# A two-layer transformer trunk: the first products of each feed-forward stage and of its last down units in another order, partial sums in another tile, the norm asked for later

## The chip, the cores and the metric

The kernel runs on 1 core of one Trainium2 chip. The metric is the time of one execution in device microseconds (us), lower is better. A core has five engines that run side by side: TensorE (PE, matmuls; its weight loads are a row of their own, PEld), VectorE (DVE), ScalarE (ACT), GpSimd (POOL) and SyncE (SP), and 16 DMA engines that carry transfers.

## The reference

Each of two layers adds half a feed-forward network, a mixer and half a second feed-forward network to x (512 tokens, 1024 features, D_FF = 2816), all in float32:

```python
def swiglu(x, w_gate, w_up, w_down):
    return (jax.nn.silu(x @ w_gate) * (x @ w_up)) @ w_down
for layer in range(DEPTH):                       # DEPTH = 2
    x = x + 0.5 * swiglu(rms_norm(x, ffn1_norm[layer]), ...)
    x = x + mixer(rms_norm(x, mix_norm[layer]))  # layer 0: pooling and attention; layer 1: gated convolution
    x = x + 0.5 * swiglu(rms_norm(x, ffn2_norm[layer]), ...)
```

The change touches only the four feed-forward networks. They are called stage 1 to stage 4 here; in the trace they lie at about 4 to 365, 555 to 905, 900 to 1250 and 1437 to 1784 us.

## The kernel before

**Data.** Activations are kept transposed, features on the 128 partitions and the 512 tokens along the free dimension. A float32 product is made of three matmuls on split operands: each operand is a high part (cast, ACT, line 87) and a low part (what the cast lost, DVE, line 88), and high times high, high times low and low times high are summed in PSUM (`mm3`, lines 214 to 217, and `product`, lines 461 to 469). Weights arrive by DMA in chunks of 128x1024 and are split in the same way into `whi` and `wlo`, three buffers each; `weights()` (line 203) hands the chunks out in the order in which products ask for them.

**A stage** (`ffn`, line 337). It begins with four "quarters" of plain products of x times the norm's gains (`xs`), 24 matmuls of 128x512 each, for the first gate and up block. Between the first two quarters it asks for the norm: `norm_columns` (line 316: token sums on PE, line 313, then 1/rms on DVE and ACT) and `norm_rows` (line 326: PE spreads the result over the partitions, line 331, and ACT copies it to the tile R, line 333). With R the normalised x (`xn`, line 371) is made, and from it seven right factors with high and low parts, the tiles fB, fT and fN (lines 380 to 400). Then unit 0's gate and up are multiplied by R, passed through silu and multiplied (t and v, lines 447 to 456).

**Units.** All other blocks are done as units of seven products P1 to P7 instead of eight (a scheme of the Strassen kind). The left factor of a product is a sum of weight blocks. The sums are formed in place by accumulating DMAs that POOL issues (line 124): in the tile `sto` P5 (src2 + src3), then P6 (+ src0, after P5 has been split), then P3 (+ src1, after P6 has been split); in the tile `ar` P1 (src0), then P7 (+ src2, after P1 has been split); in tiles `a` P2 and P4, plain loads on SP. P1, P6, P7 and P4 of a unit accumulate in one PSUM bank X, P5 and P3 in Y, P2 in Z. In a gate-up unit X is copied by ACT after P1, P6 and P7 (`copied`, lines 471 to 475): after P1 and P7 to a tile of the tag "R", that is, to the buffer that holds the norm's R at the stage's beginning; the copies are the trace's `x<-bank` at line 474. Down units add each product to x at once (DVE, line 539). In gate-up units and most down units a product has 24 matmuls of 128x256; in units 14 and 15, the two down units of the last group, 18.

**Order.** `staggered` (line 148) writes the products' order by hand: each unit's P5 and P1 lie among the products of the unit before. `full` is 13, the last gate-up unit. Units 14 and 15 are the two down units behind it and need its output: `blocks` makes the factors hz, and a split makes their parts hh (lines 87 and 88) from it. Within that order a list scheduler places instructions of all engines; each engine runs its own list in order. Where a product's weights aren't split in time, PE waits.

Of the kernel before, what the change touches and what calls it, by code (L numbers as in the profile page):

```python
# [10 lines left out]
F32 = mybir.dt.float32  # L11
# [5 lines left out]
P = 128  # L17
D = 1024
T = 512
# [22 lines left out]
def trunk(ctx: ExitStack, tc: tile.TileContext, a, out):  # L42
# [17 lines left out]
    tp = ctx.enter_context(tc.tile_pool(name="tp", bufs=2))  # L60
# [3 lines left out]
    def bank(tag="bank", bufs=None):  # L64
        return pp.tile([P, 512], F32, tag=tag, name=tag, bufs=bufs)

    def held():
        return bank("held", 2)
# [79 lines left out]
    def staggered(kinds, full):  # L148

        order = [(0, "P1"), (0, "P5")]
        for i, kind in enumerate(kinds):
            if i + 1 == len(kinds) or i == full:
                order += [(i, s) for s in ("P6", "P2", "P7", "P3", "P4")]
                order += [(i + 1, s) for s in ("P1", "P5") if i + 1 < len(kinds)]
            else:
                order += [(i, s) for s in ("P6", "P2", "P7")]
                order += [(i + 1, "P5"), (i, "P3"), (i + 1, "P1"), (i, "P4")]
        return order  # L160

    chunks = []
# [1 line left out]
    for l in range(2):  # L164
        for f in ("ffn1", "ffn2"):
# [21 lines left out]
            for kind, p in what:  # L187
                if kind == "gu":
                    units.append(seven([gu[p, q] for q in range(4)], CH, turn))
                else:  # L190
                    gi, e = p
# [4 lines left out]
            order = staggered([k for k, _ in what], max(j for j, (k, _) in enumerate(what) if k == "gu"))  # L196
# [6 lines left out]
    def weights(ahead=3, fetched=6):  # L203
        i = used[0]
        used[0] += 1
        while len(ready) < min(i + ahead, len(chunks)):
            while (loaded[0] < min(max(len(ready) + 1, i + fetched), len(chunks))
                   and chunks[loaded[0]].turn <= now[0]):
                chunks[loaded[0]].load()
                loaded[0] += 1  # L210
            ready.append(chunks[len(ready)].halves())
        return ready[i]

    def mm3(ps, wh, wl, ah, al, start, stop):
        nc.tensor.matmul(ps, wh, ah, start=start, stop=False)  # L215
        nc.tensor.matmul(ps, wh, al, start=False, stop=False)  # L216
        nc.tensor.matmul(ps, wl, ah, start=False, stop=stop)  # L217
# [11 lines left out]
    class Norm:  # L229
        acc = None  # L230
# [65 lines left out]
    def rsqrt(v, n, tag):  # L296

        s = sp.tile([P, n], F32, tag=tag + "s", name="s")
        nc.scalar.activation(s, v, AF.Sqrt)
        r0 = sp.tile([P, n], F32, tag=tag + "r", name="r0")  # L300
        nc.vector.reciprocal(r0, s)
        c = sp.tile([P, n], F32, tag=tag + "c", name="c")
        nc.vector.tensor_mul(c, r0, r0)
        nc.vector.tensor_mul(c, c, v)
        nc.vector.tensor_scalar(c, c, -0.5, 1.5, ALU.mult, ALU.add)
        r = sp.tile([P, n], F32, tag=tag, name="r")
        nc.vector.tensor_mul(r, r0, c)
        return r

    def token_sums(ps, acc):  # L310

        for i in range(NT):
            nc.tensor.matmul(ps[:, 2 * i:2 * i + 2], acc[:, i * P:(i + 1) * P], ones,
                             start=True, stop=True)

    def norm_columns():
        ps = held()
        for sq in Norm.late:
            nc.vector.tensor_add(Norm.acc, Norm.acc, sq)
        Norm.late.clear()  # L320
        token_sums(ps, Norm.acc)
        v = sp.tile([P, NT], F32, tag="nv", name="nv")
        nc.vector.tensor_scalar(v, ps[:, 0:2 * NT:2], 1.0 / D, EPS, ALU.mult, ALU.add)
        return rsqrt(v, NT, "n")

    def norm_rows(r):
        rb = tp.tile([P, NT, P], F32, tag="sq", name="rb")
        nc.vector.tensor_copy(rb, r.unsqueeze(2).broadcast_to([P, NT, P]))
        ps = held()
        for i in range(NT):  # L330
            nc.tensor.matmul(ps[:, i * P:(i + 1) * P], rb[:, i, :], ident, start=True, stop=True)
        R = tp.tile([P, T], F32, tag="R", name="R", bufs=1)
        nc.scalar.copy(R, ps)
        return R, ps


    def ffn(l, f, which, after, first=False):
        what, order = plans[l, f]
        with ExitStack() as es:
# [11 lines left out]
                begin()  # L351
            banks = [bank() for _ in range(4)]

            def quarter(outs, k0, start, stop, cut=None):
                hi, lo = weights()
                for e, ps in enumerate(outs):
                    for i in range(4):
                        s = slice((4 * e + i) * P, (4 * e + i + 1) * P)
                        mm3(ps, hi[:, s], lo[:, s], *xs[k0 + i], start and i == 0, stop and i == 3)

            quarter(banks[0:2], 0, True, False)
            r = norm_columns()
            R, Rp = norm_rows(r)
            quarter(banks[2:4], 0, True, False)
            with tc.tile_pool(name="np", bufs=1) as np_:
                xn = [np_.tile([P, 4, T], F32, tag=f"xn{e}", name=f"xn{e}") for e in range(2)]

# [101 lines left out]
                                         stop=last and i == 2, skip_group_check=True)  # L469

            def copied(ps, name):
                c = tp.tile([P, T], F32, tag="R", name=name, bufs=1) if name == "x1" else \
                    fp.tile([P, T], F32, tag=name, name=name)
                nc.scalar.copy(c, ps)  # L474
                return c
# [567 lines left out]
```

## Time and profile before

| | us |
|---|---|
| median of 3 runs (lowest to highest) | 1786.1 (1782.69 to 1787.74) |
| the profiled execution's own time | 1785.88 |
| its span | 1784.1 |
| PE busy | 1704.7 (96%) |
| PE weight load busy | 1601.1 (90%) |
| DVE busy | 1329.4 (75%) |
| ACT busy | 907.0 (51%) |
| POOL busy | 310.4 (17%) |

The span runs from the first to the last instruction. A matmul's end is modelled, so "PE busy" is not the same as PE at its peak: a PE on a lower clock is busy too. The profile therefore has to be read with the granted clock beside it.

### The profile page before, as it was taken

What the parts mean: (1) busy time and instruction counts of PE and PEld (TensorE: products, weight loads), DVE (VectorE), ACT (ScalarE), POOL (GpSimd) and SP (SyncE); (2) the same over time, 40 slices, a digit from 0 to 9 for tenths busy, and PEclk for the clock granted to TensorE, in tenths of its full rate; (3) what the DMA queues carried; (4) which work ended last, traced back from release to release, by engine and by line L of the source; (5) the groups of instructions that cost most, each with busy time, mean ns of one, the idle gap of its engine ahead of it and who ended that gap; (6) DMA issues with size and microseconds to landing.
All of it is one profiled execution on the core that took longest, in us unless ns stands there. A gap on an engine that the chain in (4) does not pass through costs nothing.

```text
span 1784.1 us, 31312 instructions
## 1 busy us (share of the span) xinstructions
PE 1704.7 (96%) x12642; PEld 1601.1 (90%) x12642; DVE 1329.4 (75%) x1891; ACT 907.0 (51%) x1300; POOL 310.4 (17%) x359
## 2 busy tenths in 40 slices
PE   8899999999999899999989999998999989999997
PEld 6899999878888899999878999998888879999997
DVE  6777786777888877786797867867755677867765
ACT  5564654564655554554555645545322345546452
POOL 2111111124202112111121111112000201111110
PEclk8899999999999899999999999999999989999999
DMA  6689989640015689989657898895332249899985
GB/s 213 157 209 217 223 212 209 141 145 25 19 48 166 154 210 212 220 214 212 143 161 172 214 225 212 209 219 122 107 102 99 95 130 214 211 221 211 222 194 113
DMA packets 89185, 303.19 MB, mean 170 GB/s; under 512 B 10704, under 2 KB 11472, under 8 KB 89040
## 3 DMA queue, kind: packets, MB, share of 16 engines
q0 software_dynamic: 36864, 130.04, 41.5%
q1 hardware_dynamic: 50512, 169.89, 27.0%
q8 instruction: 99, 1.62, 0.4%
q10 hardware_dynamic: 1664, 1.26, 0.2%
q14 instruction: 46, 0.38, 0.1%
HBM read 299.06 MB, written 2.10 MB: 169 GB/s over the span
## 4 chain that ended last, share of the span: by engine, by line
PE 80%; DVE 10%; issue 4%; ACT 3%; DMA 2%; POOL 1%; SPq 0%; ACTq 0%; DVEq 0%; POOLq 0%
PE bank L468 62%; PE bank L216 5%; PE bank L215 5%; PE bank L217 5%; DVE wlo L88 2%; ACT whi L87 1%; DMA sto<-in_ffn_w_gu 1%; DVE xn L371 1%; DVE xs L239 1%; DMA sto<-in_ffn_w_down 1%; DVE x L539 1%; DVE fT L88 1%; DVE fB L88 1%; PE bank L874 0%; PE held L215 0%
## 5 line engine op out<-in xcount | busy, mean ns | idle before, releaser
L468 PE MATMUL bank<-hh,whi 128*128 128x256 f32 x2464 | 434.3, 280 | 15.2 <-ACT whi L87 11.0
L468 PEld LDWEIGHTS bank<-hh,whi 128*128 128x128 f32 x2464 | 377.4, 190 | 19.7 <-ACT whi L87 13.6
L468 PE MATMUL bank<-hh,wlo 128*128 128x256 f32 x1232 | 344.3, 280 | 7.0 <-DVE wlo L88 7.0
L87 ACT CAST whi<-sto 128x1024 fp32r<-128x1024 f32 (+1 forms) x192 | 196.5, 1023 | 289.8 <-PE bank L468 148.7
L468 PE MATMUL bank<-fT,whi 128*128 128x256 f32 x1920 | 341.2, 281 | 0.4 <-ACT x L474 0.4
L88 DVE TENSOR_TENSOR wlo<-sto,whi 128x1024 fp32r<-128x1024 f32 (+1 forms) x192 | 228.7, 1191 | 120.0 <-ACT whi L87 119.0
L468 PEld LDWEIGHTS bank<-fT,whi 128*128 128x128 f32 x1920 | 296.1, 192 | 1.3 <-ACT x L474 1.3
L468 PE MATMUL bank<-fT,wlo 128*128 128x256 f32 x960 | 270.1, 281 | 15.5 <-DVE wlo L88 15.5
L468 PE MATMUL bank<-fN,whi 128*128 128x256 f32 x1280 | 239.0, 289 | 19.7 <-ACT x L474 15.4
L468 PEld LDWEIGHTS bank<-hh,wlo 128*128 128x128 f32 x1232 | 234.4, 191 | 8.9 <-DVE wlo L88 8.9
L468 PEld LDWEIGHTS bank<-fN,whi 128*128 128x128 f32 x1280 | 200.1, 194 | 31.9 <-ACT x L474 20.8
L468 PE MATMUL bank<-fB,whi 128*128 128x256 f32 x1280 | 228.2, 277 | 0.0
L87 ACT CAST whi<-a 128x1024 fp32r<-128x1024 f32 (+1 forms) x128 | 131.2, 1025 | 144.9 <-PE bank L468 87.0
L468 PEld LDWEIGHTS bank<-fT,wlo 128*128 128x128 f32 x960 | 184.0, 192 | 16.3 <-DVE wlo L88 16.3
L468 PEld LDWEIGHTS bank<-fB,whi 128*128 128x128 f32 x1280 | 196.1, 188 | 0.3
L88 DVE TENSOR_TENSOR wlo<-a,whi 128x1024 fp32r<-128x1024 f32 (+1 forms) x128 | 155.1, 1211 | 54.6 <-ACT whi L87 53.8
L124 POOL DMA_DIRECT2D sto<-in_ffn_w_gu x120 | 104.7, 872 | 506.3 <-DVE wlo L88 286.4
L88 DVE TENSOR_TENSOR wlo<-ar,whi 128x1024 fp32r<-128x1024 f32 (+1 forms) x128 | 152.3, 1190 | 48.3 <-ACT whi L87 48.2
L468 PE MATMUL bank<-fN,wlo 128*128 128x256 f32 x640 | 181.2, 283 | 0.0
L87 ACT CAST whi<-ar 128x1024 fp32r<-128x1024 f32 (+1 forms) x128 | 130.9, 1023 | 95.9 <-PE bank L468 52.5
L468 PE MATMUL bank<-fB,wlo 128*128 128x256 f32 x640 | 177.4, 277 | 0.0
L216 PE MATMUL bank<-xs,whi 128*128 128x512 f32 x392 | 155.0, 395 | 2.5 <-DVE xs L239 2.3
(242 smaller groups left out, 2869.6 us busy)
## 6 DMA issues: line engine op xcount, KB each, us to landing
sto<-in_ffn_w_gu POOLq DMA_DIRECT2D x120, 512.0 KB, 7.2
a<-in_ffn_w_gu SPq DMA_DIRECT2D x80, 512.0 KB, 6.6
sto<-in_ffn_w_down POOLq DMA_DIRECT2D x48, 512.0 KB, 7.5
ar<-in_ffn_w_gu SPq DMA_DIRECT2D x40, 512.0 KB, 5.4
sto<-in_ffn_w_gu SPq DMA_DIRECT2D x40, 512.0 KB, 4.6
ar<-in_ffn_w_gu POOLq DMA_DIRECT2D x40, 512.0 KB, 5.4
a<-in_ffn_w_down SPq DMA_DIRECT2D x32, 512.0 KB, 6.0
raw<-in_c_w_in SPq DMA_DIRECT2D x24, 512.0 KB, 3.5
```

The costliest lines, as they stand in the source:

```text
L87: nc.scalar.copy(hi, raw)
L88: nc.vector.tensor_sub(lo, raw, hi.bitcast(F32))
L124: nc.gpsimd.dma_start(out=self.unit[tag], in_=self.srcs[q], accum_op=ALU.add)
L215: nc.tensor.matmul(ps, wh, ah, start=start, stop=False)
L216: nc.tensor.matmul(ps, wh, al, start=False, stop=False)
L217: nc.tensor.matmul(ps, wl, ah, start=False, stop=stop)
L239: nc.vector.scalar_tensor_tensor(xl, x[k], g, xh.bitcast(F32), ALU.mult, ALU.subtract)
L371: nc.vector.scalar_tensor_tensor(xn[e][:, i], x[k], gains[:, which, k:k + 1], R if e else Rp, ALU.mult, ALU.mult)
L468: nc.tensor.matmul(o, w_[:, s], a_, start=fresh and e == 0 and k == 0 and i == 0, stop=last and i == 2, skip_group_check=True)
L539: nc.vector.scalar_tensor_tensor(o, v, 0.5 * sign, o, ALU.mult, ALU.add)
```

## The change

```diff
-        order = [(0, "P1"), (0, "P5")]
+        order = [(0, "P5"), (0, "P1")]
         for i, kind in enumerate(kinds):
-            if i + 1 == len(kinds) or i == full:
-                order += [(i, s) for s in ("P6", "P2", "P7", "P3", "P4")]
-                order += [(i + 1, s) for s in ("P1", "P5") if i + 1 < len(kinds)]
+            if i == full + 1:
+                order += [(i, s) for s in ("P1", "P5", "P2", "P6")]
+                order += [(i + 1, "P5"), (i, "P7"), (i + 1, "P1"), (i, "P3"), (i, "P4")]
             else:
                 order += [(i, s) for s in ("P6", "P2", "P7")]
-                order += [(i + 1, "P5"), (i, "P3"), (i + 1, "P1"), (i, "P4")]
+                if i + 1 == len(kinds) or i == full:
+                    order += [(i, "P3"), (i, "P4")]
+                else:
+                    order += [(i + 1, "P5"), (i, "P3"), (i + 1, "P1"), (i, "P4")]
...
-            def quarter(outs, k0, start, stop, cut=None):
+            def quarter(outs, k0, start, stop, between=None):
                 hi, lo = weights()
                 for e, ps in enumerate(outs):
+                    if e and between:
+                        between()
...
             quarter(banks[0:2], 0, True, False)
-            r = norm_columns()
-            R, Rp = norm_rows(r)
-            quarter(banks[2:4], 0, True, False)
+            rows = []
+            norm = lambda: rows.extend(norm_rows(norm_columns()))
+            quarter(banks[2:4], 0, True, False, None if first else norm)
+            if first:
+                norm()
+            R, Rp = rows
...
-                c = tp.tile([P, T], F32, tag="R", name=name, bufs=1) if name == "x1" else \
+                c = tp.tile([P, T], F32, tag="acc", name=name, bufs=1) if name == "x1" else \
```

Four parts: (1) a stage's first unit begins with P5, then P1, rather than P1, then P5. (2) Unit 14 runs P1 P5 P2 P6, unit 15's P5, P7, unit 15's P1, P3, P4, rather than P1 P5 P6 P2 P7, unit 15's P5, P3, unit 15's P1, P4. (3) X's copies after P1 and P7 go to the tile of the tag "acc", which otherwise holds the norm's sum of squares, rather than to R's. (4) The norm is asked for 12 xs matmuls later, between the halves of the second quarter; in stage 1, 24 later, behind the second quarter. Nothing is computed that wasn't before: the number of instructions is the same on every engine. Lines move by 3 (norm) or 8 (behind line 354).

**ACT at the beginning of stage 2.** `whi<-sto` is the high part of P5's weights, then of P6's, `whi<-ar` of P1's, then of P7's, `whi<-a` of P2's; `x` is X's copy. Before:

```order
L333 COPY R<-held 128x512
L87 CAST whi<-ar 128x1024
...
L87 CAST fT_6293<-hz 128x1024
L87 CAST whi<-sto 128x1024
...
L448 ACTIVATE t<-t 128x512
L87 CAST whi<-sto 128x1024
L448 ACTIVATE t<-t 128x512
L474 COPY x_6536<-bank 128x512
L87 CAST whi<-a_6425 128x1024
```

And with the change:

```order
L87 CAST whi<-sto 128x1024
L336 COPY R<-held 128x512
L87 CAST fB_6292<-xn_6395 128x1024
L87 CAST whi<-ar 128x1024
...
L87 CAST whi<-sto 128x1024
L87 CAST fN_6294<-hz 128x1024
L87 CAST whi<-a_6425 128x1024
...
L87 CAST whi<-ar 128x1024
L482 COPY x_6565<-bank 128x512
```

P5's cast now stands ahead of R's copy, and X's first copy ahead of the silu of t. In stage 3 it is so too; in stage 4 R's copy still comes first, and the cast for P5 next.

**DVE at the same place.** Before:

```order
L371 SCALAR_TENSOR_TENSOR xn_6395<-x,gains,held 128x512 x4
...
L397 SCALAR_TENSOR_TENSOR hz<-hz,xn_6396 128x1024
L88 TENSOR_TENSOR wlo<-sto,whi 128x1024
L447 TENSOR_TENSOR t<-bank,R 128x512
L88 TENSOR_TENSOR fT_6298<-hz,fT_6298 128x1024
L450 TENSOR_TENSOR v<-bank,R 128x512
...
L88 TENSOR_TENSOR wlo<-sto,whi 128x1024
```

And with the change:

```order
L88 TENSOR_TENSOR wlo<-sto,whi 128x1024
L379 SCALAR_TENSOR_TENSOR xn_6395<-x,gains,held 128x512 x4
...
L405 SCALAR_TENSOR_TENSOR hz<-hz,xn_6396 128x1024
L455 TENSOR_TENSOR t<-bank,R 128x512
L458 TENSOR_TENSOR v<-bank,R 128x512
L88 TENSOR_TENSOR fT_6298<-hz,fT_6298 128x1024
L88 TENSOR_TENSOR wlo<-sto,whi 128x1024
```

P5's low part has gone from behind line 397 to ahead of xn, and P6's, the second `wlo<-sto`, from behind both halves of the gating to behind one t, one v and one fT. In stage 4 P1's low part (`wlo<-ar`), in stages 2 and 3 among the factors, stands behind the last hz (line 405).

**DVE at unit 14 of stage 1**, where its first products meet the last gate-up unit's output; `a1` is P2's tile. Before:

```order
L439 SCALAR_TENSOR_TENSOR hz_3575<-hz_3575 128x256
L539 SCALAR_TENSOR_TENSOR x_76<-bank_3727,x_76 128x2x256
L88 TENSOR_TENSOR hh_3686<-hz_3575,hh_3686 128x512
L88 TENSOR_TENSOR wlo_3732<-sto_3577,whi_3731 128x768
L88 TENSOR_TENSOR wlo_3757<-a1_3646,whi_3756 128x768
L539 SCALAR_TENSOR_TENSOR x_76<-bank_3755,x_76 128x2x256
L88 TENSOR_TENSOR wlo_3782<-ar_3543,whi_3781 128x768
```

And with the change:

```order
L447 SCALAR_TENSOR_TENSOR hz_3575<-hz_3575 128x256
L88 TENSOR_TENSOR wlo_3732<-a1_3612,whi_3731 128x768
L88 TENSOR_TENSOR hh_3686<-hz_3575,hh_3686 128x512
L547 SCALAR_TENSOR_TENSOR x_76<-bank_3730,x_76 128x2x256
L88 TENSOR_TENSOR wlo_3758<-sto_3577,whi_3757 128x768
L547 SCALAR_TENSOR_TENSOR x_76<-bank_3754,x_76 128x2x256
L88 TENSOR_TENSOR wlo_3783<-sto_3692,whi_3782 128x768
```

P2's low part, from a plain load, now comes first, P6's third, and unit 15's P5 (`sto_3692`) ahead of P7's `ar`.

## Rows read from the trace of the kernel before

**Rows 1.** The page's part 4: the chain that ended last, by engine.

```profile
PE 80%; DVE 10%; issue 4%; ACT 3%; DMA 2%; POOL 1%; SPq 0%; ACTq 0%; DVEq 0%; POOLq 0%
```

**Rows 2.** PE's waits: us in total, times, longest us.

```profile
PE bank L468 <- DVE wlo L88: 22.5, 13, 4.2
PE bank L468 <- ACT x L474: 15.8, 12, 4.1
PE bank L468 <- ACT whi L87: 11.0, 13, 1.5
PE held L313 <- DVE acc L319: 8.9, 3, 6.7
```

**Rows 3.** Timeline of PE, stages' beginnings: start us, us, what, [idle before <-releaser].

```profile
586.98 0.58 PE L468 MATMUL bank<-fT,wlo 128*128 128x256 f32 x1 [4.16 <-DVE wlo L88]
...
595.10 0.80 PE L468 MATMUL bank<-fN,whi 128*128 128x256 f32 x2 [3.77 <-ACT x L474]
...
945.29 0.57 PE L468 MATMUL bank<-fN,whi 128*128 128x256 f32 x1 [3.19 <-ACT x L474]
...
1469.84 0.58 PE L468 MATMUL bank<-fN,whi 128*128 128x256 f32 x1 [3.11 <-ACT x L474]
```

**Rows 4.** Timeline of DVE, beginning of stage 2.

```profile
567.93 2.72 DVE L371 SCALAR_TENSOR_TENSOR xn<-x,gains,held 128x512 f32<-128x512 f32 x4 [2.85 <-ACT R L333]
...
584.57 1.22 DVE L397 SCALAR_TENSOR_TENSOR hz<-hz,xn 128x1024 f32<-128x1024 f32 x1
585.71 1.21 DVE L88 TENSOR_TENSOR wlo<-sto,whi 128x1024 fp32r<-128x1024 f32 x1
586.84 0.68 DVE L447 TENSOR_TENSOR t<-bank,R 128x512 f32<-128x512 f32 x1
...
594.08 1.22 DVE L88 TENSOR_TENSOR wlo<-sto,whi 128x1024 fp32r<-128x1024 f32 x1 [2.56 <-ACT whi L87]
```

**Rows 5.** Timeline of ACT, beginning of stage 2.

```profile
567.31 0.59 ACT L333 COPY R<-held 128x512 f32<-128x512 f32 x1 [4.03 <-PE held L331]
...
593.00 1.04 ACT L87 CAST whi<-sto 128x1024 fp32r<-128x1024 f32 x1 [4.19 <-DMA sto<-in_ffn_w_gu]
...
594.48 0.57 ACT L474 COPY x<-bank 128x512 f32<-128x512 f32 x1
```

**Rows 6.** Timeline of DVE, xn of stage 3.

```profile
918.04 1.41 DVE L371 SCALAR_TENSOR_TENSOR xn<-x,gains,held 128x512 f32<-128x512 f32 x2 [2.43 <-ACT R L333]
```

**Rows 7.** Windows, stage 2: PE, PEld, DVE, ACT, POOL busy, clock, DMA, GB/s.

```profile
572.00:576.00 4.00, 4.00 (x20) 3.30 (x19) 4.00 (x6) 2.11 (x2) 0.00 (x0) 1.00 0.54 107
```

**Rows 8.** The tile sto, 555 to 600 us (its DMA issues; time to landing).

```profile
L124 POOL DMA_DIRECT2D sto<-in_ffn_w_gu x4: 866/876/917, 565.3 to 595.7; - x4
...
DMA to landing us min/median/max: 5.2/6.5/9.5
```

**Rows 9.** Timeline of PE, the tail of stage 1 (units 14 and 15).

```profile
335.16 0.51 PE L468 MATMUL bank<-hh,whi 128*128 128x256 f32 x2 [0.82 <-ACT whi L87]
336.42 0.51 PE L468 MATMUL bank<-hh,whi 128*128 128x256 f32 x2 [0.75 <-ACT whi L87]
337.28 0.39 PE L468 MATMUL bank<-hh,wlo 128*128 128x256 f32 x1 [0.35 <-DVE wlo L88]
...
361.60 0.38 PE L468 MATMUL bank<-hh,wlo 128*128 128x256 f32 x1 [1.54 <-DVE wlo L88]
```

**Rows 10.** Timeline of ACT, P6's cast in unit 14 of stage 1.

```profile
334.28 0.83 ACT L87 CAST whi<-sto 128x768 fp32r<-128x768 f32 x1 [2.75 <-DMA sto<-in_ffn_w_down]
```

**Rows 11.** Windows in the tail of stage 1, columns as in rows 7.

```profile
338.00:342.00 4.00, 4.00 (x24) 4.00 (x24) 2.81 (x5) 0.83 (x1) 0.74 (x1) 0.60 0.78 158
342.00:346.00 4.00, 4.00 (x37) 4.00 (x36) 2.66 (x5) 1.67 (x2) 0.87 (x1) 1.00 0.65 112
334.30:361.60 27.30, 23.83 (x184) 23.17 (x183) 22.29 (x27) 14.76 (x21) 8.43 (x8) 0.94 0.54 112
```

**Rows 12.** The tile sto, 326 to 366 us.

```profile
DMA to landing us min/median/max: 4.5/5.2/5.8
```

## Prediction before the run

> **What bounds the kernel now.** I read the chain that ended last first: 80% of it is PE, 10% DVE [rows 1]. So the time is PE's work plus the places where PE waits. The list of PE's waits names those: 22.5 us for low parts (DVE, line 88), 15.8 us for X's copies (line 474), 11.0 us for high parts (ACT, line 87), 8.9 us in three waits of the token sums (line 313), one of them 6.7 us [rows 2]. PE's timeline then says where they lie. Two lie at each stage's beginning: P5's first matmul waits for its low part (4.16 us in stage 2), and P6's for X's copy (3.77, 3.19 and 3.11 us in stages 2 to 4) [rows 3]. The other cluster lies in each tail, where unit 14's P6 and P2 wait 0.82, 0.75 and 0.35 us, and unit 15's P3 waits 1.54 us at the end [rows 9]. Last I read the granted clock in windows of the tail: 0.60 from 338 to 342 us, just behind the three waits, where 24 matmuls are recorded in 4.00 us; 1.00 in the next four, with 37 [rows 11]. A gap is thus paid a second time in slow matmuls behind it. The change aims at both clusters; the reader should judge each by its own stage.
>
> The sum is made against the profiled execution, 1785.9 us with a span of 1784.1; it lies 0.2 us under the median of the three runs, so no correction is made.
>
> **The tails (part 2).** Before, P6 comes first of the products that need the last gate-up unit's output. Its weights are the last to be ready: its accumulating DMA had to wait for P5's split, its cast on ACT starts at 334.28 after 2.75 us of waiting for that DMA [rows 10]. DVE then splits P6 and only then P2, and PE, whose first wait begins at 335.16 - 0.82 = 334.34, ends both products' first pieces at 337.3 [rows 9]. By the window that follows, 24 matmuls fit from 338 to 342 [rows 11]; with the four early ones and some four between 337.3 and 338, 32 of the 36 are done by 342.0, all by about 342.6.
>
> After, P2 comes first. Its weights are a plain load, and DVE splits them before the last hh. P6 has P2's 18 matmuls as cover for its cast and split, done by about 336.1 by the same durations. With no wait, 36 matmuls at 4.00/37 = 0.108 us take 3.9 us from 334.34: 338.2. The gain is 342.6 - 338.2 = 4.4; I take 4.3. It costs nothing elsewhere: the same DMAs, casts and splits are issued, and the end wait of P3 is already there.
>
> What is late next is DVE. From 334.3 to 361.6, 27.3 us, DVE is busy 22.3 us and PE 23.8 us [rows 11]; PE's part holds about 1.4 us of slow clock (13 matmuls of 0.108 us that didn't fit between 338 and 342). So this stretch can't fall below about 22.3 on either engine: at most 5.0 can be won in it. The second thing that may be late is P3 of unit 14. Its DMA is issued when P6 is split, and between P6 and P3 lie three products (5.8 us at 0.108), against a landing of 4.5 to 5.8 us plus a cast and a split of nearly 1 us each [rows 12]. That is a tie within some 2 us. The bounds are therefore 2 and 5 per tail, against 4.3 as the likeliest, nearer to the top because the matmuls that wait are known and the tie is within the slack of P7. Four tails: 17.2, from 8 to 20.
>
> **The beginnings (parts 1, 3 and 4).** Before, P6 of stage 2 starts at 595.10 and xn at 567.93 [rows 3, 4]: 27.2 us, and in stage 3 945.29 - 918.04 = 27.2 too [rows 3, 6]. DVE runs without a break in between: the chain of factors to 585.71, then P5's low part, then the gating's t and v; P5's split starts P6's DMA, P6's cast waits 4.19 us for it until 593.00, and X's copy stands behind that cast on ACT, at 594.48 [rows 4, 5]. X's copy before also needed R free, so it couldn't go ahead of the gating.
>
> After, P5 is split ahead of xn and P6's DMA lands during the factors. P6 then needs P6's low part, which stands behind the factors (585.71 - 567.93 = 17.8 us), one t and one v (0.6 each with overlap), a fT and its own split (1.2 each) [rows 4]: 21.3 us behind xn. X's copy has no tie to R any more. If xn stayed where it is, each stage would win 27.2 - 21.3 = 5.9 us. But xn moves.
> - **Stage 1**: the norm stands behind 24 more xs matmuls. At 4.00/20 = 0.2 us each [rows 7] that is 4.8 us; one token sum still stands where it stood, so the 6.7 us wait remains [rows 2]. Its remaining slack of 1.1 us I count as 0.2, since the stage's first matmuls also wait for their first loads. Bounds 0 and 1.1.
> - **Stage 3**: 12 more xs matmuls cost 2.4; the wait ahead of line 313, of which stages 2 and 3 have 8.9 - 6.7 = 2.2 between them [rows 2], goes. Net +0.9 to +1.3. P5's cast comes ahead of R's copy here too, but ACT waits for 4 us at that place (4.03 in stage 2 [rows 5]), and in this stage POOL has little ahead of the DMA, so I take the cast to fit in. Gain 5.0; bounds 4 and 5.4, the cast being late is E.
> - **Stage 2**: P5's cast stands ahead of R's copy on ACT. P5's DMA was issued at 565.3 [rows 8]; with its load first on SP I put it 2 us earlier, 563.3. A landing took 5.2 to 9.5 us [rows 8], so the cast ends at 569.5 to 573.9 and R's copy follows instead of standing at 567.31 [rows 5]. xn moves by 2.3 to 6.6 us; I take 5.9, as the transfers at this place are the slow ones. Gain 0; bounds -0.7 and 3.6.
> - **Stage 4**: R's copy still comes first, but P1's split stands behind all factors: 18.9 us behind xn. P7's DMA follows (5.2 to 6.5 [rows 8]), then its cast (1.0) and, behind it on ACT, X's copy (0.6): 25.7 to 27 us. With xn 1.4 later and five matmuls of P2 drawn ahead (0.5 us), the result is -0.5; bounds -1.5 and 2.
>
> Sum 0.2 + 0 + 5.0 - 0.5 = 4.7, from about 2 to 12.
>
> Part 3 by itself costs nothing: the tag's old user, the norm's sum, is read last before the factors begin, and the next norm's sums start when the gate-ups are done. P1 and P5 swapped adds no work either.
>
> **Sum.** 17.2 + 4.7 = 21.9; 1785.9 - 21.9 = **1764.0**.
>
> **One rule against the change.** POOL's DMAs in the tail landed in 4.5 to 5.8 us while DVE was busy 22.3 of 27.3 us [rows 11, 12], so a busy DVE did not visibly hold them. The Trainium skill ("SBUF — State Buffer", the box on DVE blocking a DMA) says that a DMA issued by GpSimd can starve for descriptors while VectorE holds the port the two share. A tail that is denser on DVE would then make every accumulating DMA later, which is case B by another road; the rows speak against it so far.
>
> **The rivals.**
> - **B, the tails give half back.** P3 of unit 14 and the last P3 wait for DVE and for the accumulating DMA, so that only 2 us per tail remain: 8 + 4.7 = 12.7, 1773. For it: the tie above, and DVE at 22.3 of a possible 23. Against it: the landings in this tail are short [rows 12]. Chance 0.17.
> - **C, everything comes at its upper bound.** Tails 4 x 5 = 20, beginnings 12: 32, 1754. For it: stage 2's landing could be as short as 5.2 us, the shortest of that tile. Chance 0.18.
> - **D, no change that a measurement can tell** (within 0.3%, 5.4 us; a run of this kernel can't tell less). The order of PE's waits only changes: unit 14's P6 waits in its new place as long as P6 and P2 did, and P6 of the stages starts 27 us behind xn for another reason, the DMA of P7. 1784. Against it: P2's weights need no DMA sum. Chance 0.06.
> - **E, slower.** ACT's cast of P5 holds R's copy, and with it xn and everything behind it, until an accumulating DMA lands. It decides when that DMA delays R's copy by over 13.7 us more than I take it to in each of stages 2 and 3, since 2 x 13.7 = 27.3 is the forecast gain and 5.4 more. At 17 us: 1764 + 34 = 1798. No landing in the rows took more than 9.5 us [rows 8]. Chance 0.04.
>
> **How the numbers follow.** A, the forecast, has 0.55, with a range of its own from 1758 (tails 5.0, beginnings 8) to 1770 (tails 3.3, beginnings 2.7). To hold 8 in 10 the range takes in C's centre and most of B: 1754 to 1776. Faster by over 0.3% are A, B and C: 0.90; within 0.3% D: 0.06; slower E: 0.04.
>
> **What would show it right or wrong.** Tails: no wait over 0.5 us between P1 and P7 of unit 14, and a clock of 1.00 behind it. Beginnings: P6 starts 21.3 us behind xn in stages 1 to 3, and about 26 in stage 4; the token sums' wait shrinks from 8.9 to 6.7. In stage 2 ACT waits for `sto` ahead of R's copy. Wrong would be: a wait of over 2 us ahead of unit 14's P3; P6 still waiting for X's copy in stage 3; R's copy in stage 3 held by P5's cast.

## The result

The changed kernel took 1765.7 us (median of 4 runs, 1761.67 to 1768.79) where the kernel before took 1786.9 us beside it (median of 4, 1782.69 to 1788.9): a ratio of 0.9883, 95% interval 0.9855 to 0.9911. That is 1.2% faster; the forecast was 1764.0 in a range of 1754 to 1776. The profiled execution of the changed kernel is the slowest of its four, 1768.79 us, so the profiled spans differ by 17.1 us where the medians differ by 21.2.

The head of the page after, which answers to the table of before:

```profile
span 1767.0 us, 31319 instructions
...
PE 1697.0 (96%) x12642; PEld 1594.4 (90%) x12642; DVE 1328.1 (75%) x1891; ACT 906.9 (51%) x1300; POOL 312.0 (18%) x359
```

No engine does less work. PE's waits after (us in total, times, longest), beside [rows 2]:

```profile
PE bank L476 <- DVE wlo L88: 15.8, 8, 4.8
PE bank L476 <- ACT x L482: 11.2, 13, 3.2
PE bank L476 <- ACT whi L87: 6.8, 8, 1.0
PE held L316 <- DVE acc L322: 6.7, 1, 6.7
PE bank L476 <- DVE t L455: 4.1, 2, 3.6
```

The low parts' share falls from 22.5 to 15.8 us, the high parts' from 11.0 to 6.8, X's copies' from 15.8 to 11.2; a new one, for the gating's t, comes with 4.1.

**The tails.** PE's timeline of stage 1's tail after, beside [rows 9]:

```profile
332.24 0.39 PE L476 MATMUL bank<-hh,whi 128*128 128x256 f32 x1 [0.45 <-DVE hh L88]
...
357.60 0.39 PE L476 MATMUL bank<-hh,wlo 128*128 128x256 f32 x1 [1.58 <-DVE wlo L88]
```

Between the wait for the last factors at 332.24 and the last P3 there is none; the waits of 0.82, 0.75 and 0.35 us are gone. The windows of this tail (columns as in rows 7):

```profile
333.00:337.00 4.00, 4.00 (x36) 3.87 (x35) 3.51 (x7) 2.39 (x4) 0.00 (x0) 1.00 0.67 165
337.00:341.00 4.00, 4.00 (x35) 3.97 (x35) 4.00 (x6) 1.48 (x2) 1.75 (x2) 1.00 0.54 76
334.70:357.60 22.90, 21.30 (x183) 20.76 (x182) 20.60 (x27) 13.45 (x19) 9.15 (x8) 1.00 0.64 133
```

The clock stays at 1.00 where it was 0.60 for four us before, and 36 matmuls fit in four us where 24 did. The stretch from the first matmul behind unit 14's P1 and P5 to the last P3, 27.3 us before [rows 11], is 22.9 here with as many matmuls (183 against 184). DVE is busy for 20.6 us of it, against 22.3 of the longer stretch. P3's wait for DVE, 1.58 us, stands where one of 1.54 stood.

**The beginnings.** Stage 2 after, on ACT, DVE and PE:

```profile
571.88 1.05 ACT L87 CAST whi<-sto 128x1024 fp32r<-128x1024 f32 x1 [8.44 <-DMA sto<-in_ffn_w_gu]
572.96 0.59 ACT L336 COPY R<-held 128x512 f32<-128x512 f32 x1
...
623.31 1.05 ACT L87 CAST whi<-sto 128x1024 fp32r<-128x1024 f32 x1 [3.43 <-DMA sto<-in_ffn_w_gu]
```

```profile
574.11 2.72 DVE L379 SCALAR_TENSOR_TENSOR xn<-x,gains,held 128x512 f32<-128x512 f32 x4
...
594.23 1.22 DVE L88 TENSOR_TENSOR wlo<-sto,whi 128x1024 fp32r<-128x1024 f32 x1
```

```profile
591.79 0.80 PE L476 MATMUL bank<-fN,whi 128*128 128x256 f32 x2 [3.19 <-ACT x L482]
595.50 0.58 PE L476 MATMUL bank<-fN,wlo 128*128 128x256 f32 x1 [2.08 <-DVE wlo L88]
610.36 0.51 PE L476 MATMUL bank<-fT,whi 128*128 128x256 f32 x2 [1.03 <-ACT whi L87]
625.41 0.50 PE L476 MATMUL bank<-fT,whi 128*128 128x256 f32 x2 [1.39 <-ACT x L482]
```

ACT waits 8.44 us for P5's accumulating DMA with R's copy behind it; xn starts at 574.11. P6's split starts 20.1 us behind xn and ends 21.3 behind it, as computed, and P6's bulk runs from 595.50, where the whole of P6 ran from 595.10 before [rows 3]. Behind it two more waits follow, 1.03 and 1.39 us, both put down to ACT, which the kernel before didn't have there. In the second ACT is held again: its cast at 623.31 waits 3.43 us for an accumulating DMA, and X's copy stands behind that cast. Stage 3, where nothing holds R's copy, shows the same 20.1 us on DVE; P6's bulk there is 21.4 us behind xn, 5.9 less than P6 before [rows 3, 6]. P6's first two matmuls there still wait for X's copy, 2.30 us (3.19 before [rows 3]):

```profile
918.11 2.72 DVE L379 SCALAR_TENSOR_TENSOR xn<-x,gains,held 128x512 f32<-128x512 f32 x4
...
938.23 1.22 DVE L88 TENSOR_TENSOR wlo<-sto,whi 128x1024 fp32r<-128x1024 f32 x1
```

```profile
935.62 0.51 PE L476 MATMUL bank<-fN,whi 128*128 128x256 f32 x2 [2.30 <-ACT x L482]
...
939.50 0.58 PE L476 MATMUL bank<-fN,wlo 128*128 128x256 f32 x1 [2.07 <-DVE wlo L88]
```

**The balance.** The timelines of PE and DVE give a ledger. A beginning is counted from the end of the last product matmul of the stage before (for stage 1 from 0) to the first add to x of a down unit (line 539 before, 547 after), so those of stages 2 and 4 hold the mixers. A tail is counted from the last gate-up matmul to the end of the last product. All in us of the profiled executions; the rest of the span is the body of the stages.

```
                    beginnings, stages 1 to 4       sum   tails, stages 1 to 4       sum    span
before              129.5  303.0  113.1  289.4    835.0   37.1  37.0  36.7  38.2   149.0  1784.1
after               128.7  309.7  109.7  288.3    836.4   32.4  32.3  32.8  30.6   128.1  1767.0
tail_alone          127.9  302.4  112.8  288.2    831.3   32.3  32.2  32.4  30.2   127.1  1756.6
begin_alone         128.9  305.2  109.5  289.1    832.7   36.6  36.1  35.8  33.7   142.3  1774.3
p6_first            128.3  308.2  109.5  287.2    833.1   36.5  36.4  36.4  35.2   144.5  1776.4
swap_only           129.1  302.4  114.5  289.1    835.1   33.8  33.2  33.6  33.0   133.6  1769.2
p1_first            130.5  299.5  110.8  289.7    830.6   32.3  32.8  32.1  30.3   127.4  1758.5
copies_r            131.2  305.1  110.7  286.9    833.9   32.3  32.2  32.4  30.1   126.9  1762.6
late_alone          131.8  299.0  111.4  291.6    833.7   36.3  36.9  36.1  34.4   143.6  1780.6
tail_acc            129.0  301.5  111.9  289.5    831.8   32.2  32.3  32.3  31.0   127.8  1758.1
norm_early          125.2  301.9  112.5  285.2    824.8   32.3  32.3  32.1  30.0   126.7  1749.9
early_r             125.0  299.3  109.8  284.7    818.8   32.9  32.9  32.8  30.9   129.5  1745.8
hybrid              127.2  299.5  109.7  289.0    825.4   32.3  32.3  32.2  29.9   126.7  1753.9
best                124.5  298.1  109.7  286.6    818.9   32.2  32.2  32.2  30.0   126.5  1748.1
```

From before to after, the tails win 20.9 us, the beginnings lose 1.4 and the rest 2.4: together the 17.1 by which the span is shorter. So the change is its tails. How far such rows can be trusted is seen in kernels that share a part. Tails of the new order agree within 1.1 us. Those of the four kernels with P6 ahead of P2 agree within 1 us in stages 1 to 3, but in stage 4 the kernel before has 38.2 where begin_alone, late_alone and p6_first have 33.7 to 35.2. The beginnings of one arrangement differ by up to 4 us in the sum, and the rest, in which the kernels differ only by the tile of X's copies, lies between 797.5 and 803.3. Stage 2's beginning holds the mixer of layer 0, which was slower in this execution after (in the last section).

### The profile page after: what moved, and what is told of

It is laid out like the page before. It is cut to its first block, busy times and chain, and to the rows that moved or that the text cites. A ratio compares the mean times of both kernels' runs of the same rounds, so it can differ in the third digit from the quotient of the medians.

```text
span 1767.0 us, 31319 instructions
## 1 busy us (share of the span) xinstructions
PE 1697.0 (96%) x12642; PEld 1594.4 (90%) x12642; DVE 1328.1 (75%) x1891; ACT 906.9 (51%) x1300; POOL 312.0 (18%) x359
## 3 DMA queue, kind: packets, MB, share of 16 engines
q1 hardware_dynamic: 50512, 169.89, 27.2%
## 4 chain that ended last, share of the span: by engine, by line
PE 80%; DVE 10%; issue 3%; ACT 3%; DMA 3%; POOL 1%; SPq 0%; ACTq 0%; DVEq 0%; POOLq 0%
PE bank L476 61%; PE bank L218 5%; PE bank L219 5%; PE bank L220 5%; DMA sto<-in_ffn_w_gu 2%; DVE wlo L88 2%; ACT whi L87 1%; DVE xn L379 1%; DVE xs L242 1%; DVE fT L88 1%; DVE fB L88 1%; PE bank L882 0%; PE held L218 0%; PE held L219 0%; PE held L220 0%
## 5 line engine op out<-in xcount | busy, mean ns | idle before, releaser
L476 PE MATMUL bank<-hh,whi 128*128 128x256 f32 x2464 | 429.9, 278 | 7.3 <-ACT whi L87 3.9
L476 PEld LDWEIGHTS bank<-fT,whi 128*128 128x128 f32 x1920 | 292.1, 189 | 11.2 <-ACT whi L87 3.5
```

The costliest lines, as they stand in the source:

```text
L476: nc.tensor.matmul(o, w_[:, s], a_, start=fresh and e == 0 and k == 0 and i == 0, stop=last and i == 2, skip_group_check=True)
```

## The experiments

Each comparison is with the kernel before on the same chip; ratios carry their 95% interval. Edits are against the changed kernel, except where the text says that they are against the kernel before.

**1. The tail's order alone** (tail_alone): the kernel before with the loop of `staggered` that the change has, and nothing else.

```diff
...
+            if i == full + 1:
+                order += [(i, s) for s in ("P1", "P5", "P2", "P6")]
+                order += [(i + 1, "P5"), (i, "P7"), (i + 1, "P1"), (i, "P3"), (i, "P4")]
...
```

> Only part 2 (the order of unit 14's products) is put into the kernel before. Theory: the tails carry the whole gain, because P2's plain load is ready while P6's accumulating DMA, cast and split run under P2's matmuls. Then PE has no wait between P1 and P7 of unit 14, the tails are shorter by 4.0 to 4.7 us in stages 1 to 3 and about 7 in stage 4 as in the changed kernel, and the time is about 1766 us (1762 to 1770). Rival: the beginnings (P5 first, copies in acc, late norm) carry it, and the tail's gain is given back to DVE: 1780 us or more.

Measured: 1766.4 us, 0.9885 (0.9863 to 0.9907), as the whole change. The tails sum to 127.1 us, 21.9 less than before. The theory holds: the tails alone are worth what the whole change is worth.

**2. The beginnings alone** (begin_alone): parts 1, 3 and 4 with the order of unit 14 as before.

```diff
-            if i == full + 1:
...
+            if i + 1 == len(kinds) or i == full:
+                order += [(i, s) for s in ("P6", "P2", "P7", "P3", "P4")]
...
```

> Parts 1, 3 and 4 (P5 first, copies in the acc tile, late norm) without part 2. Theory: what stages 3 and 4 win (about 5 us together) stage 2 loses, where R's copy waits on ACT behind P5's cast for the accumulating DMA: 1787 us (1783 to 1790), and the three waits of each tail are back. Rival (beginnings carry the gain): 1775 us or less.

Measured: 1778.3 us, 0.9959 (0.9944 to 0.9975): between the two, 4.7 us under the theory's range. The beginnings themselves give 2.3 us (835.0 to 832.7), and R's copy is held as in the changed kernel:

```profile
571.41 1.05 ACT L87 CAST whi<-sto 128x1024 fp32r<-128x1024 f32 x1 [8.55 <-DMA sto<-in_ffn_w_gu]
572.48 0.59 ACT L333 COPY R<-held 128x512 f32<-128x512 f32 x1
```

But the tails, whose order is the old one, are 6.7 us shorter too, 4.5 of them in stage 4. The tile sto's time to landing there, before and in this kernel:

```profile
DMA to landing us min/median/max: 4.7/4.7/8.0
```

```profile
DMA to landing us min/median/max: 4.2/4.9/6.1
```

A landing of 8.0 us, which the last products of before waited for, is missing. Why it landed late there, and whether it does so in every execution, is open: there is one profile of the kernel before. If it does, it would explain why the parts don't add: 19 us by the tail alone and 7 by the beginnings alone, but 21 together, since either part takes stage 4's late landing off the path. That is argued and not shown.

**3. P6 ahead of P2 again** (p6_first):

```diff
-                order += [(i, s) for s in ("P1", "P5", "P2", "P6")]
+                order += [(i, s) for s in ("P1", "P5", "P6", "P2")]
```

> The changed kernel with P6 ahead of P2 in unit 14 again, unit 15's P5 still ahead of P7. Theory: the waits for P6's cast and split come back ahead of P6 and P2, 1.9 us per tail with the slow clock behind them, and the time is 1777 to 1783 us. Rival: the gain comes from unit 15's P5 and P1 being drawn forward, by which the accumulating DMAs of unit 15 start earlier: 1764 to 1770 us as the changed kernel.

Measured: 1776.7 us, 0.9946 (0.9924 to 0.9967), 0.3 us under the theory's range and far from the rival's. The waits are back in stage 1's tail:

```profile
333.51 0.50 PE L476 MATMUL bank<-hh,whi 128*128 128x256 f32 x2 [0.58 <-ACT whi L87]
334.76 0.50 PE L476 MATMUL bank<-hh,whi 128*128 128x256 f32 x2 [0.75 <-ACT whi L87]
335.49 0.67 PE L476 MATMUL bank<-hh,whi 128*128 128x256 f32 x2 [0.23 <-ACT whi L87]
...
359.49 0.39 PE L476 MATMUL bank<-hh,wlo 128*128 128x256 f32 x1 [1.65 <-DVE wlo L88]
```

and the tails sum to 144.5 us, 16.4 more than after. With the same beginnings and unit 15's P5 behind P7, begin_alone has 142.3 us of tails and 0.9959: unit 15's P5 drawn ahead of P7 brings nothing by itself.

**4. P2 and P6 exchanged and nothing more** (swap_only), against the kernel before:

```diff
...
+                order += [(i, s) for s in ("P1", "P5", "P2", "P6")]
+                order += [(i, "P7"), (i + 1, "P5"), (i, "P3"), (i + 1, "P1"), (i, "P4")]
...
```

> The kernel before with nothing but P2 put ahead of P6 in unit 14; unit 15's P5 and P1 stay where they were, behind P7 and P3. Theory: the exchange of P2 and P6 alone is the tail's gain; PE has no wait between P1 and P7 of unit 14, the tails are about 32.5 us each and the time is 1766 us (1762 to 1771). Rival: unit 15's P5 drawn ahead of P7 is needed too, since P7 then comes 18 matmuls too early for its split; a wait ahead of P7 or P3 stands in the tails and the time is 1772 to 1778 us.

Measured: 1774.1 us, 0.9935 (0.9914 to 0.9956). Here the rival was right. The tails sum to 133.6 us: the exchange wins 15.4 of the 21.9 us that tail_alone wins, and PE still waits ahead of P7 and, a little longer than before, ahead of the last P3:

```profile
338.46 0.38 PE L471 MATMUL bank<-hh,wlo 128*128 128x256 f32 x1 [0.49 <-DVE wlo L88]
357.73 0.38 PE L471 MATMUL bank<-hh,wlo 128*128 128x256 f32 x1 [1.81 <-DVE wlo L88]
```

The wait ahead of P7, 0.3 to 0.5 us, stands in all four tails; with unit 15's P5 ahead of P7 (run 1) it stands in none. Both halves of part 2 are needed.

**5. P1 first** (p1_first):

```diff
-        order = [(0, "P5"), (0, "P1")]
+        order = [(0, "P1"), (0, "P5")]
```

> The changed kernel with P1 ahead of P5 at a stage's beginning again (part 1 undone). Theory: in stage 2 ACT casts P1's plain load ahead of R's copy and waits for no accumulating DMA; the 8.4 us wait of ACT goes, xn starts some 5 us earlier and P6 with it, stage 3 stays as it is, stage 4 loses 1 to 3 us since P6 stands behind both halves of the gating again: 1760 us (1757 to 1765). Rival: P5 first is what shortens the beginnings, and without it P6 is 27 us behind xn everywhere: 1770 to 1775 us.

Measured: 1763.3 us, 0.9877 (0.9859 to 0.9896): in the theory's range, though the ratios don't tell it from the changed kernel. On ACT in stage 2 the cast ahead of R's copy waits for no DMA now:

```profile
562.07 1.05 ACT L87 CAST whi<-ar 128x1024 fp32r<-128x1024 f32 x1 [2.30 <-PE bank L219]
563.83 0.59 ACT L336 COPY R<-held 128x512 f32<-128x512 f32 x1 [0.70 <-PE held L334]
```

and stage 2's beginning falls from 309.7 to 299.5. Stages 1 and 4 lose 1.8 and 1.4, stage 3 loses 1.1.

**6. Copies in R's buffer** (copies_r), part 3 undone:

```diff
-                c = tp.tile([P, T], F32, tag="acc", name=name, bufs=1) if name == "x1" else \
+                c = tp.tile([P, T], F32, tag="R", name=name, bufs=1) if name == "x1" else \
```

> The changed kernel with X's copies after P1 and P7 back in R's buffer (part 3 undone). Theory: X's copy must wait until both halves of the gating have read R, which stand behind P6's and P2's splits now, so P6 starts later than its split allows, some 27 to 30 us behind xn in stages 1 to 3 instead of 21; 2 to 6 us per stage are lost: 1772 us (1768 to 1780). Rival: the acc tile does nothing, since P6 waits for its low part anyway: 1765.7 us as the changed kernel, within 2.

Measured: 1765.1 us, 0.9886 (0.9859 to 0.9912), the same as the changed kernel. The theory falls, though the delay that it named is there: P6's bulk is 25.7 to 26.0 us behind xn in stages 1 to 3, 4.3 to 4.6 more than after. PE runs more of P2 meanwhile, and no time is lost. Part 3 is worth nothing that can be measured, and how far P6 stands behind xn doesn't by itself set the time.

**7. The norm asked for early** (norm_early), part 4 undone:

```diff
-            quarter(banks[2:4], 0, True, False, None if first else norm)
-            if first:
-                norm()
-            R, Rp = rows
+            R, Rp = norm_rows(norm_columns())
+            quarter(banks[2:4], 0, True, False)
```

> The changed kernel with the norm asked for between the first two quarters again (part 4 undone). Theory: R's copy stands ahead of P5's cast on ACT, xn in stage 2 starts where it did before (about 202 us behind stage 1's end, 7 us earlier than in the changed kernel without the mixer's share), but X's copy stands behind P7's cast, whose DMA starts only after the factors, so P6 starts 26 us behind xn in stages 2 to 4: stage 2 wins 2 to 5 us, stage 3 loses 2 to 4, 1765 us (1761 to 1769). Rival: the late norm is what shortens stages 2 and 3, so that without it the time is 1770 us or more.

Measured: 1753.1 us, 0.9821 (0.9795 to 0.9848), 12 us under the theory's 1765, 8 under its range, and clear of the changed kernel's interval: both expectations missed. Part 4 costs the changed kernel some 11 us by the ratios: the beginnings sum to 824.8 us against 836.4, by 3.5 us less in stage 1, 7.8 in stage 2, 3.1 in stage 4, and 2.8 more in stage 3.

**8. A beginning chosen for each stage** (hybrid): stages 1 and 4 as before, stage 2 with P1 first, copies in acc and the late norm, stage 3 as in the changed kernel.

```diff
+                              ("P5", "P1") if (l, f) == (1, "ffn1") else ("P1", "P5"))
...
+                c = tp.tile([P, T], F32, tag="acc" if which in (2, 3) else "R", name=name, bufs=1) if name == "x1" else \
...
+            late = which in (2, 3)
+            if not late:
+                norm()
+            quarter(banks[2:4], 0, True, False, norm if late else None)
...
```

> Each stage's beginning is chosen from the runs so far: stages 1 and 4 as before (P1 first, copies in R, early norm), stage 2 with P1 first, copies in acc and the late norm, stage 3 as in the changed kernel; the tails as in the changed kernel. Theory: the stages' gains add, since each beginning is bounded by its own chain from xn: about 3 us in stage 2 and 3 in stage 3 over the tails alone (1766.4), 1760 us (1756 to 1763). Rival: what a stage wins at its beginning it gives back in waits for splits and copies of the next units, or runs vary by more than this: 1763 us or more.

Measured: 1755.9 us, 0.984 (0.9814 to 0.9866): just under the theory's range. Stage 2's beginning is that of run 5 (299.5), stage 3's that of the changed kernel (109.7), and those of stages 1 and 4 are within 0.8 us of run 1: the stages' beginnings add within what they vary by.

**9. The late norm alone** (late_alone), part 4 put into the kernel before.

```diff
-            r = norm_columns()
-            R, Rp = norm_rows(r)
-            quarter(banks[2:4], 0, True, False)
+            rows = []
+            norm = lambda: rows.extend(norm_rows(norm_columns()))
+            quarter(banks[2:4], 0, True, False, None if first else norm)
+            if first:
+                norm()
+            R, Rp = rows
```

> The kernel before with nothing but the late norm (part 4). Theory: asking later delays xn by 5 us in stage 1 and by about 1 us in each other stage, and P6 stays 25 to 27 us behind xn since X's copies wait for R; what is left is the delay: 1790 us (1787 to 1795). Rival: the late norm only hurts together with P5 first, whose cast on ACT then stands ahead of R's copy; alone it is free: 1783 to 1786 us.

Measured: 0.9983 (0.9967 to 0.9999), 1778.6 us where the kernel before took 1782.3 beside it. The theory's loss isn't there; the rival's "alone it is free" fits, though the time is 4.4 us under its range too; the kernel before was 3.4 us or more faster here than beside runs 1 to 8. In stage 2 R's copy isn't held, since P1's plain load is cast ahead of it, and stage 2's beginning is 299.0; stage 1 loses 2.3 and stage 4 2.2.

**10. Parts 2 and 3** (tail_acc): P1 first, early norm, copies in acc.

```diff
-        order = [(0, "P5"), (0, "P1")]
+        order = [(0, "P1"), (0, "P5")]
...
+            R, Rp = norm_rows(norm_columns())
+            quarter(banks[2:4], 0, True, False)
...
```

> Parts 2 and 3 alone: the tail's order and X's copies in acc, with P1 first and the early norm. Theory: with P1 first P5's split stands behind all factors, P6's DMA starts only then and P6 is 27 us behind xn as before, wherever X's copy goes: 1766 us as the tail alone (1762 to 1769), 13 more than with P5 first. Rival: it is X's free copy and not P5 first that brought the early-norm kernel to 1753: 1752 to 1757 us.

Measured: 1761.2 us, 0.9878 (0.9859 to 0.9897). By the ratio this is the tail alone, as the theory had it; its 1761 is 0.8 us under the stated range, and the kernel before was 3.6 us faster beside it than beside tail_alone. The copy's buffer isn't what brought norm_early to 1753.

**11. Parts 1 and 2** (early_r): P5 first and the tail's order, the norm early, the copies in R.

```diff
-                c = tp.tile([P, T], F32, tag="acc", name=name, bufs=1) if name == "x1" else \
+                c = tp.tile([P, T], F32, tag="R", name=name, bufs=1) if name == "x1" else \
...
+            R, Rp = norm_rows(norm_columns())
+            quarter(banks[2:4], 0, True, False)
...
```

> Parts 1 and 2 alone: P5 first and the tail's order, with the early norm and X's copies in R (the early-norm kernel with part 3 undone). Theory: P6's split still ends some 22.5 us behind xn, X's copy moves only by one silu on ACT (0.6 us) because it already stood behind P7's cast; beginnings lose under 1 us per stage: 1754 us (1751 to 1758). Rival: the copy's buffer matters, P6 falls back to 27 us or more behind xn: 1762 us or more.

Measured: 1750.4 us, 0.9818 (0.98 to 0.9836), 0.6 under the range. It beats both kernels and is smaller than the change. The step of the theory was wrong all the same: in stage 2 P6's split ends 24.8 us behind xn and not 22.5, and P6 starts 29.3 behind it, as the rival had it, without costing what the rival said. PE's timeline of stage 2 first:

```profile
569.65 0.38 PE L472 MATMUL bank<-fT,wlo 128*128 128x256 f32 x1 [0.24 <-DVE wlo L88]
578.74 0.58 PE L472 MATMUL bank<-fB,wlo 128*128 128x256 f32 x1 [6.08 <-DVE wlo L88]
584.01 0.38 PE L472 MATMUL bank<-fB,wlo 128*128 128x256 f32 x1 [0.28 <-DVE wlo L88]
586.61 0.51 PE L472 MATMUL bank<-fN,whi 128*128 128x256 f32 x2 [0.50 <-ACT x L478]
```

Then the windows from P5's first matmul over 36 us, of this kernel and of the changed one (columns as in rows 7):

```profile
569.00:605.00 36.00, 28.71 (x219) 27.30 (x218) 33.80 (x45) 22.88 (x30) 6.09 (x7) 0.91 0.61 140
```

```profile
579.80:616.00 36.20, 28.40 (x195) 27.25 (x196) 32.84 (x43) 20.26 (x26) 4.34 (x5) 0.81 0.45 98
```

There is one long wait, 6.08 us, in P1, where the changed kernel has four: 2.22 and 1.36 us in P5, 3.19 and 2.08 at P6. While X's copy and P6's split are still being made, PE runs 18 of P2's 24 matmuls; P6 waits 0.50 us and all its 24 matmuls follow in one piece. In the changed kernel only two of P2's matmuls stand there, and P6 is torn into 2 and 22 with a wait on each side. So 219 matmuls are done in 36.0 us against 195 in 36.2, at a mean clock of 0.91 against 0.81. DVE is busy 33.8 of the 36.0 us.

P2's matmuls ahead of P6 aren't what decides, though. The four kernels with P5 first and the new tails, by norm and by the tile of X's copies (counts and distances in stage 2, P6 from its third matmul on):

```
                          P2's matmuls   P6 behind   xn behind         beginnings,
                          ahead of P6    xn          stage 1's end     sum           ratio
after       late, acc           2          21.4        212.4             836.4       0.9883
copies_r    late, R            10          25.7        208.7             833.9       0.9886
norm_early  early, acc          5          29.4        201.1             824.8       0.9821
early_r     early, R           18          29.6        201.3             818.8       0.9818
```

The ratio goes with the norm, that is, with xn, and neither with the order of P2 and P6 nor with P6's distance from xn. What early_r has over norm_early in the beginnings, 6.0 us of two executions, its ratio doesn't show.

**12. A beginning chosen for each stage, with P5 first in stages 1 and 4** (best): hybrid with stages 1 and 4 as in norm_early.

```diff
+                              ("P1", "P5") if (l, f) == (0, "ffn2") else ("P5", "P1"))
...
+            late = which in (2, 3)
+            if not late:
+                norm()
+            quarter(banks[2:4], 0, True, False, norm if late else None)
...
```

> The early-norm kernel in stages 1 and 4 (P5 first, acc, norm as before), stage 2 with P1 first and the late norm, stage 3 as in the changed kernel; tails as in the changed kernel. Theory: stages add: 2.4 us in stage 2 and 2.8 in stage 3 over the early-norm kernel by the profiled beginnings: 1749 us (1745 to 1752). Rival: the stages' differences of 2 to 3 us are within what one kernel varies by from run to run: 1752 to 1757 us.

Measured: 1750.8 us, 0.983 (0.9811 to 0.9849). By the median it is in the theory's range, but no better than early_r, whose two parts do the same without a choice by stage.

## Why the prediction was right, and where it wasn't

**The sum** came out, in part by luck: 21.9 us were forecast, 21.2 measured between medians. Its two terms were off in opposite directions. In the profiled executions the tails gave 20.9 us, not 17.2; the beginnings lost 1.4 where 4.7 were to be won; the rest, which had no term, lost 2.4.

**The tails.** The mechanism is shown by runs 1, 3 and 4: P2's plain load is ready, and its matmuls cover P6's DMA, cast and split. In all four tails the waits of P6 and P2 are there in each kernel with P6 ahead of P2 and in none with P2 ahead. 4.3 us per tail were forecast; stages 1 to 3 gave 4.7, 4.7 and 3.9, within the bounds, and stage 4 gave 7.6, over the upper one of 5.0. That excess comes with the landing of 8.0 us in the one profile of before: against the three other kernels that run P6 ahead of P2 (33.7 to 35.2 us) stage 4 gives 3.1 to 4.6, and the four tails together 16 to 18. So the term was sized well, or short by stage 4's landing; which of the two is open.

The sum gave nothing of the tails to unit 15's P5 ahead of P7. Run 4 shows that it has a share: the exchange of P2 and P6 alone wins 15.4 us of tails, both together 21.9. The floor of 22.3 us for the stretch to the last P3, DVE's busy time in it before, wasn't one: in the new order DVE has 20.6 us of work there. What remains late is DVE, as forecast: ahead of the last P3's split in stage 1 it works without a break from 349.3 us on, and P3 waits 1.58 us for that split.

**The rule against the change** (the Trainium skill, "SBUF — State Buffer", the box on DVE blocking a DMA) was taken to make the accumulating DMAs of a denser tail late. That box of the Trainium skill speaks of DVE instructions in a mode that locks GpSimd out of the port pair the two share. Whether DVE's instructions in this tail run in such a mode, no run here shows. The trace of the changed kernel speaks against the effect in this tail: with DVE busy 20.6 of 22.9 us, against 22.3 of 27.3 before, the tile sto's landings took

```profile
DMA to landing us min/median/max: 4.9/5.5/6.9
```

against 4.5, 5.2 and 5.8 before [rows 12]. That is 0.3 us later at the median, and no wait came of it but P3's old one. Rival B was wrong.

**The beginnings.** The steps that held are the chain on DVE, P6's split ending 21.3 us behind xn in stages 2 and 3, as worked out; xn of stage 1 starting 4.9 us later (28.8 to 33.7), as 24 more xs matmuls at 0.2 us gave; and the token sums' wait falling from 8.9 to 6.7. By stage 0.2, 0, 5.0 and -0.5 were forecast; 0.8, -6.7, 3.4 and 1.1 were measured. The steps that failed are two:
- "xn moves by 2.3 to 6.6 us; I take 5.9" in stage 2. It started 212.4 us behind stage 1's end where it was 202.2; 2.9 of the 10.2 lie in the mixer (from stage 1's end to PE's wait for the attention's p, 161.7 us before and 164.7 after), so xn moved by 7.3, beyond the bound. P5's accumulating DMA took 10.1 us to land, where 5.2 to 9.5 were allowed for. That is rival E's mechanism at a smaller price. Counted from the end of that wait, xn stands at 40.5 us with the early norm (before, runs 1, 4, 7, 10 and 11), at 41.7 with the late norm and P1 first (runs 5, 8, 9 and 12), and at 47.7 to 48.3 with the late norm and P5 first (after, runs 2, 3 and 6): the later norm alone costs 1.2 us there, the held copy 6 or more.
- "If xn stayed where it is, each stage would win 27.2 - 21.3 = 5.9 us": P6's distance from xn was taken for time. Runs 6, 7 and 11 show that it isn't. With P6 25.7 us behind xn the time is the same, and with P6 29 us behind an early xn it is some 11 us less by the ratios; PE has P2's matmuls to run meanwhile. "X's copy has no tie to R any more" didn't free P6 either: in stage 3 its first two matmuls still wait 2.30 us for the copy, which was named as a sign of being wrong. Of the 5.9 us by which P6's bulk came nearer to xn there, 3.4 were left in the stage's beginning.

"Part 3 by itself costs nothing" was right, and it brings nothing either (run 6, run 10 against 1, and run 11 against 7). Part 4 was charged with a delay of xn in each stage, and P5 first was credited only with what was left after that delay; run 7 shows what it brings without: with parts 1 to 3 and the early norm the gain is some 32 us and not 21. In stage 2 the held copy is part of the difference; what the late norm costs in stages 1 and 4 with P5 first (3.5 and 3.1 us) and why it costs nothing over all with P1 first (run 9) wasn't traced.

## What to carry to other kernels

Where several products wait for the same new operand, the one whose other operand is ready first should come first, and one that depends on nothing new should stand behind it: run 4 shows that the first without the second is seven tenths of what the tails win. Before a step is moved later, look at what an engine that runs its list in order then has ahead of the instruction that starts the longest chain: a cast that waited for a DMA ahead of a copy of 0.6 us cost 6. The distance between two steps is no measure of the time, as long as the engine has other work to put between them. And undo each part of a change that has several: here one of four parts carried the whole gain, one was worth nothing, and two cancelled each other: by the ratios P5 first wins 10 to 12 us with the early norm and none with the late one.

## What the runs showed of the hardware that wasn't expected

- At the same granted clock of 1.00 PE ran in stretches at two paces. Over the same 20 us of stage 1 the kernel before and the changed one had

```profile
120.00:140.00 20.00, 19.90 (x175) 19.70 (x175) 16.70 (x24) 11.61 (x16) 3.48 (x4) 1.00 0.89 214
```

```profile
120.00:140.00 20.00, 20.00 (x170) 19.82 (x169) 16.52 (x23) 11.63 (x16) 3.49 (x4) 1.00 0.88 207
```

  175 matmuls against 170 with no idle time of more than 0.1 us on either side. This is part of what the changed kernel's profiled execution lost outside its beginnings and tails. What sets the pace is open.
- The granted clock fell in the mixer of layer 0 in the profiled execution after where it didn't before, though the change doesn't touch that code. Before, then after:

```profile
404.00:408.00 4.00, 4.00 (x25) 3.62 (x24) 2.36 (x10) 2.47 (x15) 0.56 (x2) 1.00 0.28 70
```

```profile
400.00:404.00 4.00, 4.00 (x18) 3.50 (x17) 1.95 (x7) 2.17 (x14) 0.35 (x1) 0.57 0.26 68
```

  The mixers are shifted by 4 us against each other, so the two windows hold the same place: 25 matmuls at 1.00, 18 at 0.57. Stage differences of 2 to 3 us that hold a mixer should be trusted only where several kernels show them.
